# Delta-net mixer: squares ordered key first, pair scales on VectorE, two of four diagonal block copies on GpSimd, and E blocks placed ahead of the block copies into KQ

## The chip, the cores and the metric

The kernel runs on one core of a Trainium2 chip. The metric is device time in microseconds (us). The core has five instruction queues that run side by side, each strictly in its own order: PE (TensorE, the matrix engine; the profile shows its weight loads apart as PEld), DVE (VectorE), ACT (ScalarE), POOL (GpSimd) and SP (SyncE, which here only issues DMAs). An instruction that has to wait for a semaphore holds up everything that stands behind it in the same queue. [...]

## The reference

A two-layer encoder trunk over 256 positions of width 1024. Each layer is a SwiGLU block, a mixer, and a second SwiGLU block, each between RMS norms. The mixer of layer 0 is a short convolution, that of layer 1 a gated delta net. Only the delta net is touched by the change:

```python
CHUNK = 64
k_beta = k * beta[..., None]
a = jnp.where(strict, einsum("bhncd,bhnsd->bhncs", k_beta, k) * decay, 0.0)
t_inv = triangular_solve(eye + a, eye, left_side=True, lower=True)
u = einsum("bhncs,bhnse->bhnce", t_inv, v_beta)
qk = jnp.where(causal, einsum("bhncd,bhnsd->bhncs", q, k) * decay, 0.0)
...
v_new = u_n - einsum("bhcd,bhde->bhce", w_n, state)
o = einsum("bhcd,bhde->bhce", q_g_n, state) + einsum("bhcs,bhse->bhce", qk_n, v_new)
```

q and k are normalised per head (8 key heads, each used by two of the 16 value heads), so the sum of squares of each key and query row is needed; t_inv is the inverse of a unit triangular matrix for each head and each piece of the sequence. The output is the trunk's result, 256 x 1024 in float32.

## The kernel before

**Number format and units.** Products are made at float32 accuracy from a rounded part and a residual. Each weight block of 128 x 1024 (a "unit") is brought in by SP's queue (three raw buffers), rounded by ACT (`whi`, L119), and its residual made by DVE (`wlo`, L121); eight pairs of `whi` and `wlo` exist at a time. PE multiplies twice or three times per block: L221, L222 and L225 in a group of 24 matmuls with 512 columns (`act_group`), L278 to L280 in a group of 24 with 256 columns (`stat_group`).

**The delta-net stage** runs in this order of code: head slabs, then nine tiles of keys and queries (`stat_group`), three z groups (`z_group`, six tiles of 24 matmuls: 144), four v groups (`v_group`, 16 tiles), and the last z group. Other work is threaded into this as chains: Python generators that a ticker resumes every few matmuls, so that a chain's instructions are recorded between those of the large products. A list scheduler then fixes the order on each engine: from what it takes to be ready it picks what was recorded first. The order that stands in each queue in the end can therefore differ from the code's, and the order of one engine can move when another's work changes.

**`kq_chain`** (L605) goes over four groups of two key heads. For a head it transposes keys and queries on PE (L618), multiplies keys with keys and queries (L621), both into PSUM buffers named `acc` of which there are four, copies parts out on ACT (L624, L625) and makes sums of squares on ACT (L630, a square with accumulation, four for each head). For a group POOL adds a small constant (L634), DVE takes the reciprocal (L636), POOL makes the pair scales `dsc` (L639), and DVE makes eight scaled products with the decay into the tile `KQ` (L645, four for each half t of the sequence). ACT then copies the four 32 x 32 diagonal blocks of each half into `Ld` (L652, 32 copies in all). POOL makes three more small tiles from the sums (L654, L656, L658).

**`invert`** (L667) starts when all four groups are done. DVE transposes `Ld` (L669), inverts all the 32 x 32 blocks at once by 31 steps of two instructions (L677, L679), each of which needs the one before, and transposes the result twice (`Xd`, L681, and `Yd`, L683). POOL copies the inverted blocks back into `KQ` (L689, 32 copies). After `yield INV_WAIT`, the inverse of the larger blocks is built in two halves of eight heads: PE multiplies with `Xd` (L707), ACT copies out (L711), PE again (L718, L719), ACT copies into the tiles `E` and `KQ` (L722, L726), and so on to L742. `E` is filled beforehand by POOL from `Xd` (L699, L700).

**`v_pair`** and **`scan`** follow: a convolution of v on DVE (`yb`, L586), a SiLU on ACT (L573), transposes on PE (L757), and the solve with `KQ` on PE (L771).

Of the kernel before, what the change touches and what calls it, by code (L numbers as in the profile page):

```python
# [7 lines left out]
F32 = mybir.dt.float32  # L8
F32R = mybir.dt.float32r
AF = mybir.ActivationFunctionType  # L10
ALU = mybir.AluOpType
# [38 lines left out]
def trunk_kernel(ctx: ExitStack, tc: tile.TileContext, x, norm_g, w_gu, w_dn, sc_in, sc_cw, sc_out,  # L50
# [76 lines left out]
    def slab(shape, dtype, name):  # L127
        return hp.tile(shape, dtype, name=name, tag="slab")
# [347 lines left out]
    def gdn_proj(xh, xl, mid):  # L476
# [128 lines left out]
        def kq_chain():  # L605

            for gi in range(NG):
                ss = sp.tile([P, NT, 2, 2], F32, name="kss", bufs=2)
                k1 = slab([P, 2, 2, P], F32, "kq1")
                pkq = []  # L610
                for i in range(2):
                    kh = 2 * gi + i
                    while kq[kh] is None or tk.now < kq_time[kh] + KQ_WAIT:
                        yield 1
                    tp = side_bank().rearrange("p (t c) d -> p t c d", t=NT)
                    for t in range(NT):
                        for c in range(2):
                            PE.transpose(tp[:, t, c, :], kq[kh][:, c, t * P:(t + 1) * P], ident)  # L618
                    pk = side_bank().rearrange("p (t c) d -> p t c d", t=NT)
                    for t in range(NT):  # L620
                        PE.matmul(pk[:, t, :, :], lhsT=kq[kh][:, 0, t * P:(t + 1) * P],  # L621
                                  rhs=kq[kh][:, :, t * P:(t + 1) * P], start=True, stop=True)
                    pkq.append(pk)
                    S.activation(ktok[:, kh, :], tp[:, 0, 0, :], AF.Copy)  # L624
                    S.activation(k1[:, i, :, :], kq[kh][:, :, P:], AF.Copy)  # L625
                    kq1[kh] = k1[:, i, :, :]
                    for t in range(NT):
                        for c in range(2):
                            junk = sp.tile([P, 512], mybir.dt.bfloat16, name="junk", bufs=1)
                            S.activation(junk[:, 0:P], tp[:, t, c, :], AF.Square, accum_out=ss[:, t, c, i:i + 1])  # L630
                    yield 1
                while dec[1][gi] is None:
                    yield 1
                G.tensor_scalar(ss, ss, EPS, None, ALU.add)  # L634
                rk = sp.tile([P, NT, 2], F32, name="rk", bufs=2)
                V.reciprocal(rk, ss[:, :, 0, :])  # L636
                dd = small(f"dsc{gi}", 8).rearrange("p (t n) -> p t n", t=NT)
                for t in range(NT):
                    G.tensor_tensor(dd[:, t, :].rearrange("p (k v) -> p k v", k=2),  # L639
                                    beta[:, t, 4 * gi:4 * gi + 4].rearrange("p (k v) -> p k v", k=2),  # L640
                                    rk[:, t, :].unsqueeze(2).broadcast_to([P, 2, 2]), ALU.mult)
                for t in range(NT):
                    m = big([P, 4, 2, P], F32, "KQ")
                    for hv in range(4):
                        V.scalar_tensor_tensor(m[:, hv, :, :], pkq[hv // 2][:, t, :, :], dd[:, t, hv:hv + 1],  # L645
                                               bc(dec[t][gi][:, hv, :], 2), ALU.mult, ALU.mult)
                    KQ[gi][t] = m
                    for b in range(4):
                        r = slice(b * B32, (b + 1) * B32)
                        o = Ld[r, :, 8 * gi + t:8 * gi + t + 7:2].rearrange("p i v -> p v i")  # L650
                        i_ = m[r, :, 0, b * B32:(b + 1) * B32]
                        S.activation(o, i_, AF.Copy)  # L652
                n = small(f"nk{gi}", 4).rearrange("p (t n) -> p t n", t=NT)
                G.tensor_tensor(n, ss[:, :, 0, :], phalf.rearrange("p (t n) -> p t n", t=NT), ALU.pow)  # L654
                q = small(f"eq{gi}", 4).rearrange("p (t n) -> p t n", t=NT)
                G.tensor_scalar(q, ss[:, :, 1, :], 128.0 * EPS, None, ALU.mult)  # L656
                w = small(f"wt{gi}", 4)
                G.tensor_tensor(w, etail[:, 4 * gi:4 * gi + 4], dd[:, 0, :], ALU.mult)  # L658
                Dsc[gi], nk[gi], eq[gi], wt[gi] = dd, n, q, w
                yield 1  # L660
            tk.start(invert())


# [3 lines left out]
        def invert():  # L667
# [14 lines left out]
            Yd = row("blk").rearrange("p (a b) -> p a b", a=B32)  # L682
            V.transpose(Yd.rearrange("p h i -> p i h"), X)  # L683
            T1 = row("blk").rearrange("p (a b) -> p a b", a=B32)
            for gi in range(NG):
                for t in range(NT):
                    for b in range(4):
                        r = slice(b * B32, (b + 1) * B32)
                        G.tensor_copy(KQ[gi][t][r, :, 0, r], Yd[r, 8 * gi + t:8 * gi + t + 7:2, :])  # L689
            yield INV_WAIT  # L690
            for half in range(2):
                hs = slice(16 * half, 16 * half + 16)
                gis = (2 * half, 2 * half + 1)
                E = {}
                for gi in gis:
                    E[gi] = slab([P, 8, 64], F32, "E64")
                    for b in range(2):
                        r = slice(b * B32, (b + 1) * B32)
                        G.tensor_copy(E[gi][r, :, r], Xd[r, 8 * gi:8 * gi + 8, :])  # L699
                    G.memset(E[gi][0:B32, :, B32:], 0.0)  # L700
                pt = side_bank().rearrange("p a (b c) -> p (a b) c", c=B32)
                for x in range(16):
                    ht = 16 * half + x
                    m = KQ[ht // 8][ht % 2]
                    for b in (0, 2):
                        r0, r1 = slice(b * B32, (b + 1) * B32), slice((b + 1) * B32, (b + 2) * B32)
                        PE.matmul(pt[r1, x, :], lhsT=m[r0, (ht // 2) % 4, 0, r1], rhs=Xd[r0, ht, :],  # L707
                                  start=True, stop=True)
                for b in (1, 3):
                    r = slice(b * B32, (b + 1) * B32)  # L710
                    S.activation(T1[r, hs, :], pt[r], AF.Copy)  # L711
                yield 1
                py = side_bank().rearrange("p a (b c) -> p (a b) c", c=B32)
                for x in range(16):
                    ht = 16 * half + x
                    for b in (0, 2):
                        r0, r1 = slice(b * B32, (b + 1) * B32), slice((b + 1) * B32, (b + 2) * B32)
                        PE.matmul(py[r0, x, :], lhsT=T1[r1, ht, :], rhs=Yd[r1, ht, :], start=True, stop=True)  # L718
                    PE.matmul(py[B32:64, x, :], lhsT=Yd[B32:64, ht, :], rhs=T1[B32:64, ht, :], start=True, stop=True)  # L719
                for gi in gis:  # L720
                    x0 = 8 * (gi % 2)
                    S.activation(E[gi][B32:64, :, 0:B32], py[B32:64, x0:x0 + 8, :], AF.Copy, scale=-1.0)  # L722
                    for t in range(NT):
                        for b in (0, 2):
                            r0, r1 = slice(b * B32, (b + 1) * B32), slice((b + 1) * B32, (b + 2) * B32)
                            S.activation(KQ[gi][t][r0, :, 0, r1], py[r0, x0 + t:x0 + t + 7:2, :], AF.Copy, scale=-1.0)  # L726
                yield 1
                lo, up = slice(0, 64), slice(64, P)
                for gi in gis:
                    pz = side_bank().rearrange("p a (b c) -> p (a b) c", c=64)  # L730
                    for x in range(8):
                        PE.matmul(pz[up, x, :], lhsT=KQ[gi][x % 2][lo, x // 2, 0, up], rhs=E[gi][lo, x, :],
                                  start=True, stop=True)
                    S.activation(E[gi][up], pz[up], AF.Copy)
                yield 1
                for gi in gis:
                    pw = side_bank().rearrange("p a (b c) -> p (a b) c", c=64)
                    for x in range(8):
                        PE.matmul(pw[lo, x, :], lhsT=E[gi][up, x, :], rhs=KQ[gi][x % 2][up, x // 2, 0, up],
                                  start=True, stop=True)  # L740
                    for t in range(NT):
                        S.activation(KQ[gi][t][lo, :, 0, up], pw[lo, t:t + 7:2, :], AF.Copy, scale=-1.0)  # L742
                    inv_done[gi] = True
# [312 lines left out]
```

## Time and profile before

| | |
|---|---|
| median of 3 runs | 1127.42 us (1125.82 to 1130.31) |
| the profiled execution | 1128.42 us |
| its span, first to last instruction | 1126.5 us |
| DVE busy in the span | 749.9 us (67%) |
| ACT busy in the span | 651.8 us (58%) |
| POOL busy in the span | 88.8 us (8%) |
| mean granted TensorE clock | 0.995 |
| delta-net stage, from head slabs to the last z group | about 660 to 930 us of the span |

Times in the timeline are counted from the start of the span. The time of the program is 1.9 us longer than the span of the same execution, which lies ahead of the first and behind the last instruction. Durations of PE overlap, since matmuls are pipelined: how fast they go is read from the distance between starts. A bracket at the end of a timeline row gives how long the engine sat idle before that instruction, and the instruction that ended the wait.

### The profile page before, as it was taken

Reading aid. Unit: us, or ns where it says so; the run is one execution under the profiler, and the core shown is the slowest. Engines: PE = TensorE matmul, PEld = TensorE weight load, DVE = VectorE, ACT = ScalarE, POOL = GpSimd, SP = SyncE. Lnnn points to the kernel's source line nnn. Section 1 sums busy time; section 2 is a strip of 40 time slices with the busy share of each in tenths; the row PEclk is TensorE's granted clock in tenths of the full one; section 3 lists DMA queues with packets and bytes.
Section 4 is the critical chain, followed back from the end, with each engine's and each line's share of the span. In section 5 each row is a group of like instructions: output and inputs, shape, how many; then the busy total and the mean of one; then the engine's idle time right before and its main releaser. Section 6 shows DMA issues by size and latency. Waiting matters only on the chain.

```text
span 1126.5 us, 16842 instructions
## 1 busy us (share of the span) xinstructions
PE 1100.2 (98%) x6284; PEld 942.4 (84%) x6284; DVE 749.9 (67%) x1140; ACT 651.8 (58%) x1201; POOL 88.8 (8%) x167
## 2 busy tenths in 40 slices
PE   9999999999999999999999999889899999999997
PEld 6888887888788888788888877778899887888886
DVE  7776735687777663577765468768946557767543
ACT  6666535545556653556664358784587645666432
POOL 0100000000200000010000012110141212000000
PEclk9999999999999999999999999999999999999999
DMA  8755555656566565576555653327332355655552
GB/s 271 244 185 190 191 166 167 225 180 198 182 223 204 171 206 165 163 229 209 189 185 169 193 185 113 94 94 227 114 129 76 131 168 168 213 199 190 185 168 75
DMA packets 55955, 198.12 MB, mean 176 GB/s; under 512 B 6721, under 2 KB 7233, under 8 KB 55874
## 3 DMA queue, kind: packets, MB, share of 16 engines
q1 hardware_dynamic: 55728, 196.99, 54.2%
q8 instruction: 49, 0.80, 0.3%
q14 instruction: 32, 0.26, 0.1%
q10 hardware_dynamic: 146, 0.07, 0.0%
HBM read 195.99 MB, written 1.05 MB: 175 GB/s over the span
## 4 chain that ended last, share of the span: by engine, by line
PE 81%; DVE 7%; ACT 5%; DMA 3%; issue 2%; POOL 2%; SPq 0%; DVEq 0%; POOLq 0%; ACTq 0%
PE mm L298 27%; PE mm L301 14%; PE acc L324 7%; PE acc L325 7%; PE acc L323 7%; PE mm L221 3%; PE mm L222 3%; PE mm L225 3%; DVE wlo L121 2%; ACT whi L119 1%; ACT blk L652 1%; DVE kq L586 1%; PE mm L176 1%; ACT junk L147 1%; DMA raw<-in_w_gu 1%
## 5 line engine op out<-in xcount | busy, mean ns | idle before, releaser
L121 DVE TENSOR_TENSOR wlo<-raw,whi 128x1024 fp32r<-128x1024 f32 (+2 forms) x362 | 437.5, 1220 | 240.2 <-ACT whi L119 201.5
L119 ACT ACTIVATE whi<-raw 128x1024 fp32r<-128x1024 f32 (+2 forms) x362 | 376.1, 1051 | 224.3 <-PE acc L325 104.6
L298 PE MATMUL mm<-x,whi 128*128 128x512 f32 x1312 | 329.4, 393 | 0.0
L298 PEld LDWEIGHTS mm<-x,whi 128*128 128x128 f32 x1312 | 235.9, 189 | 42.4
L301 PEld LDWEIGHTS mm<-x,wlo 128*128 128x128 f32 x1312 | 179.0, 190 | 12.8
L301 PE MATMUL mm<-x,wlo 128*128 128x256 f32 x1312 | 182.9, 282 | 0.0
L323 PE MATMUL acc<-whi,hb 128*128 128x512 f32 x352 | 136.5, 388 | 0.0
L324 PE MATMUL acc<-wlo,hb 128*128 128x512 f32 x352 | 135.6, 385 | 0.3 <-DVE wlo L121 0.3
L325 PE MATMUL acc<-whi,hb 128*128 128x512 f32 x352 | 135.3, 385 | 0.0
L308 ACT ACTIVATE corr<-mm 128x256 f32<-128x256 f32 x164 | 61.2, 376 | 67.4 <-PE mm L301 65.6
L221 PE MATMUL mm<-whi,x 128*128 128x512 f32 (+1 forms) x240 | 94.4, 394 | 0.9 <-ACT x L178 0.7
L222 PE MATMUL mm<-wlo,x 128*128 128x512 f32 (+1 forms) x240 | 94.2, 393 | 0.7 <-DVE wlo L121 0.7
L225 PE MATMUL mm<-whi,x 128*128 128x512 f32 (+1 forms) x240 | 87.8, 389 | 0.2 <-DVE x L179 0.2
L324 PEld LDWEIGHTS acc<-wlo,hb 128*128 128x128 f32 x352 | 66.2, 188 | 13.8 <-DVE wlo L121 0.8
L323 PEld LDWEIGHTS acc<-whi,hb 128*128 128x128 f32 x352 | 66.2, 188 | 13.1
L325 PEld LDWEIGHTS acc<-whi,hb 128*128 128x128 f32 x352 | 66.1, 188 | 13.2
L154 POOL TENSOR_SCALAR rstd<-ss 128x1 f32<-128x1 f32 x24 | 12.3, 513 | 786.1 <-ACT junk L147 786.1
L278 PE MATMUL mm<-x,whi 128*128 128x256 f32 x200 | 59.7, 299 | 2.0 <-DVE kq L586 2.0
L279 PE MATMUL mm<-x,whi 128*128 128x256 f32 x200 | 58.4, 292 | 0.0
L280 PE MATMUL mm<-x,wlo 128*128 128x256 f32 x200 | 57.9, 289 | 0.0
L222 PEld LDWEIGHTS mm<-wlo,x 128*128 128x128 f32 x240 | 45.2, 188 | 11.2 <-DVE wlo L121 2.9
L221 PEld LDWEIGHTS mm<-whi,x 128*128 128x128 f32 x240 | 45.2, 188 | 11.1 <-ACT x L178 2.7
(216 smaller groups left out, 1238.3 us busy)
## 6 DMA issues: line engine op xcount, KB each, us to landing
raw<-in_w_gu SPq DMA_DIRECT2D x176, 512.0 KB, 4.2
raw<-in_w_dn SPq DMA_DIRECT2D x88, 512.0 KB, 3.6
raw<-in_sc_in SPq DMA_DIRECT2D x24, 512.0 KB, 4.1
raw<-in_gdn_z SPq DMA_DIRECT2D x16, 512.0 KB, 3.9
raw<-in_gdn_v SPq DMA_DIRECT2D x16, 512.0 KB, 4.2
raw<-in_gdn_out SPq DMA_DIRECT2D x16, 512.0 KB, 3.7
gamma<-in_norm_g SPq DMA_DIRECT2D x11, 512.0 KB, 5.4
raw<-in_gdn_a SPq DMA_DIRECT2D x9, 512.0 KB, 4.4
```

The costliest lines, as they stand in the source:

```text
L119: S.activation(hi[:, r], raw[:, r], AF.Copy)
L121: newest[0] = V.tensor_tensor(lo[:, r], raw[:, r], hi[:, r], ALU.subtract).ins
L221: PE.matmul(pt, lhsT=xh[:, t, k, :], rhs=hi, start=(k == 0), stop=False)
L222: PE.matmul(pt, lhsT=xh[:, t, k, :], rhs=lo, start=False, stop=False)
L225: PE.matmul(pt, lhsT=xl[:, t, j, :], rhs=part(j)[0], start=False, stop=(j == KD - 1))
L278: PE.matmul(ptile, lhsT=hi, rhs=h2, start=(k == 0), stop=False)
L298: PE.matmul(flat, lhsT=part(k, 0), rhs=xx[:, k].rearrange("p h t q -> p (h t q)"), start=(k == 0), stop=False)
L301: PE.matmul(flat[:, T:], lhsT=part(k, 1), rhs=xx[:, k, 0].rearrange("p t q -> p (t q)"), start=False, stop=(k == KD - 1))
L308: S.activation(c, pt[:, 1, :], AF.Copy)
L323: PE.matmul(o, lhsT=yh(c, t), rhs=hi[:, r], start=(c == 0), stop=False)
L324: PE.matmul(o, lhsT=yh(c, t), rhs=lo[:, r], start=False, stop=False)
L325: i = PE.matmul(o, lhsT=yl(c, t), rhs=hi[:, r], start=False, stop=(c == n - 1)).ins
```

## The change

Four edits, all in `gdn_proj`:

1. In `kq_chain` the sums of squares stand ahead of the two copies out of PSUM, and both key squares (c = 0) ahead of both query squares (c = 1). The tile `ss` has its axes swapped, so that the key sums lie together.
2. Adding the small constant to the key sums and making the pair scales `dsc` move from POOL to DVE. The query sums get the constant in the instruction that makes `eq`.
3. Of the four diagonal block copies of each half, ACT keeps two and POOL makes two: 16 copies and 16 copies.
4. In `invert` the copies into `E` are recorded ahead of the copies into `KQ`, half by half, with an explicit order on POOL's queue; before, all 32 copies into `KQ` were recorded first.

```diff
-                ss = sp.tile([P, NT, 2, 2], F32, name="kss", bufs=2)
+                ss = sp.tile([P, 2, NT, 2], F32, name="kss", bufs=2)
...
+                    for c in range(2):
+                        for t in range(NT):
+                            junk = sp.tile([P, 512], mybir.dt.bfloat16, name="junk", bufs=1)
+                            S.activation(junk[:, 0:P], tp[:, t, c, :], AF.Square, accum_out=ss[:, c, t, i:i + 1])
                     S.activation(ktok[:, kh, :], tp[:, 0, 0, :], AF.Copy)
                     S.activation(k1[:, i, :, :], kq[kh][:, :, P:], AF.Copy)
                     kq1[kh] = k1[:, i, :, :]
-                    for t in range(NT):
-                        for c in range(2):
-                            junk = sp.tile([P, 512], mybir.dt.bfloat16, name="junk", bufs=1)
-                            S.activation(junk[:, 0:P], tp[:, t, c, :], AF.Square, accum_out=ss[:, t, c, i:i + 1])
...
-                G.tensor_scalar(ss, ss, EPS, None, ALU.add)
+                V.tensor_scalar(ss[:, 0], ss[:, 0], EPS, None, ALU.add)
                 rk = sp.tile([P, NT, 2], F32, name="rk", bufs=2)
-                V.reciprocal(rk, ss[:, :, 0, :])
+                V.reciprocal(rk, ss[:, 0])
                 dd = small(f"dsc{gi}", 8).rearrange("p (t n) -> p t n", t=NT)
                 for t in range(NT):
-                    G.tensor_tensor(dd[:, t, :].rearrange("p (k v) -> p k v", k=2),
+                    V.tensor_tensor(dd[:, t, :].rearrange("p (k v) -> p k v", k=2),
...
-                        S.activation(o, i_, AF.Copy)
+                        if b < 2:
+                            S.activation(o, i_, AF.Copy)
+                        else:
+                            G.tensor_copy(o, i_)
...
-                G.tensor_scalar(q, ss[:, :, 1, :], 128.0 * EPS, None, ALU.mult)
+                G.tensor_scalar(q, ss[:, 1], EPS, 128.0 * EPS, ALU.add, ALU.mult)
...
-            for gi in range(NG):
-                for t in range(NT):
-                    for b in range(4):
-                        r = slice(b * B32, (b + 1) * B32)
-                        G.tensor_copy(KQ[gi][t][r, :, 0, r], Yd[r, 8 * gi + t:8 * gi + t + 7:2, :])
+            E, placed = {}, [None]
+
+            def place(half):
+
+                gis = (2 * half, 2 * half + 1)
+                for gi in gis:
+                    E[gi] = slab([P, 8, 64], F32, "E64")
...
+                            G.tensor_copy(E[gi][r, :, r], Xd[r, 8 * gi:8 * gi + 8, :])
...
+                                last = G.tensor_copy(KQ[gi][t][r, :, 0, r], Yd[r, 8 * gi + t:8 * gi + t + 7:2, :]).ins
+                placed[0] = last
+
+            place(0)
             yield INV_WAIT
             for half in range(2):
...
+                if half:
+                    place(1)
```

**What the edits move in the queues.** The scheduler gives other orders on PE, ACT, DVE and POOL through the whole delta-net stage; SP's is the same. Three places matter. Line numbers of the changed kernel are up to 16 higher: L723 is the old L707, L684 and L686 the old L681 and L683, L680 and L682 the old L677 and L679, L653 and L655 the old L652, L727 the old L711, L773 and L787 the old L757 and L771.

First PE, where the first products with the inverted blocks stand (`acc<-blk,KQ`). Before, they stand in the v groups (L278 to L280), behind all 144 matmuls of the z groups and 228 of the v groups:

```order
L278 MATMUL mm<-x_5783,whi 128x256
L279 MATMUL mm<-x_5783,whi 128x256
L280 MATMUL mm<-x_5783,wlo 128x256
L707 MATMUL acc<-blk,KQ 32x32 x32
L278 MATMUL mm<-x_5783,whi 128x256
L279 MATMUL mm<-x_5783,whi 128x256
```

Of the change, the same engine and products: they stand ahead of the last tile of the three z groups (L221 to L225).

```order
L221 MATMUL mm<-whi,x_5783 128x512
L222 MATMUL mm<-wlo,x_5783 128x512
L225 MATMUL mm<-whi,x_5783 128x512
L723 MATMUL acc<-blk,KQ 32x32 x32
L221 MATMUL mm<-whi,x_5783 128x512
L222 MATMUL mm<-wlo,x_5783 128x512
```

So 24 matmuls of 512 columns, 228 of 256 columns and three sets of four transposes of v (old L757) have moved from ahead of these products to behind them. What they wait for is the first transpose of the inverse on DVE (old L681).

Second DVE in the middle of the inversion (`blk` and `sg`). Before, the convolutions of v (`yb`) and the residuals (`wlo`) stand between its steps, 20 and 18 of them up to the first transpose of the result:

```order
L677 TENSOR_TENSOR sg<-blk 128x247
L586 SCALAR_TENSOR_TENSOR yb<-mm,gcw,yb 128x255
L679 TENSOR_TENSOR blk<-blk,sg 128x13x19
L586 SCALAR_TENSOR_TENSOR yb<-mm,gcw,yb 128x254
L677 TENSOR_TENSOR sg<-blk 128x240
L586 SCALAR_TENSOR_TENSOR yb<-mm,gcw,yb 128x253
```

Of the change, the end of the inversion on DVE:

```order
L680 TENSOR_TENSOR sg<-blk 128x31
L682 TENSOR_TENSOR blk<-blk,sg 128x31
L684 STREAM_TRANSPOSE blk<-blk 128x32x32
L686 STREAM_TRANSPOSE blk<-blk 128x32x32
L121 TENSOR_TENSOR wlo<-raw,whi 128x1024 x4
L586 SCALAR_TENSOR_TENSOR yb<-mm,gcw,yb 128x255
```

The convolutions of v now all stand behind the inversion, and of the residuals eight stand inside it, all in its first ten steps.

Third ACT, from the last head's squares (`junk,kss`) to the end of the z groups' SiLUs (`zs`). Before:

```order
L573 ACTIVATE zs<-mm 128x512
L119 ACTIVATE whi<-raw 128x1024
L652 ACTIVATE blk<-KQ 32x4x32 x4
L119 ACTIVATE whi<-raw 128x1024
L652 ACTIVATE blk<-KQ 32x4x32 x4
L119 ACTIVATE whi<-raw 128x1024
L573 ACTIVATE zs<-mm 128x512
```

Of the change:

```order
L119 ACTIVATE whi<-raw 128x1024
L653 ACTIVATE blk<-KQ 32x4x32 x2
L119 ACTIVATE whi<-raw 128x1024
L653 ACTIVATE blk<-KQ 32x4x32 x2
L119 ACTIVATE whi<-raw 128x1024 x7
L573 ACTIVATE zs<-mm 128x512 x4
L727 ACTIVATE blk<-acc 32x512 x2
L119 ACTIVATE whi<-raw 128x1024 x3
```

The copy out of the first products (L727) now stands ahead of the next three roundings of weights.

More of the change, by code (lines that the diff above doesn't have):

```diff
@@ L651, in kq_chain @@
                         i_ = m[r, :, 0, b * B32:(b + 1) * B32]
-                        S.activation(o, i_, AF.Copy)
+                        if b < 2:
+                            S.activation(o, i_, AF.Copy)
+                        else:
+                            G.tensor_copy(o, i_)
                 n = small(f"nk{gi}", 4).rearrange("p (t n) -> p t n", t=NT)
-                G.tensor_tensor(n, ss[:, :, 0, :], phalf.rearrange("p (t n) -> p t n", t=NT), ALU.pow)
+                G.tensor_tensor(n, ss[:, 0], phalf.rearrange("p (t n) -> p t n", t=NT), ALU.pow)
                 q = small(f"eq{gi}", 4).rearrange("p (t n) -> p t n", t=NT)
-                G.tensor_scalar(q, ss[:, :, 1, :], 128.0 * EPS, None, ALU.mult)
+                G.tensor_scalar(q, ss[:, 1], EPS, 128.0 * EPS, ALU.add, ALU.mult)
                 w = small(f"wt{gi}", 4)
@@ L684, in invert @@
             T1 = row("blk").rearrange("p (a b) -> p a b", a=B32)
-            for gi in range(NG):
-                for t in range(NT):
-                    for b in range(4):
-                        r = slice(b * B32, (b + 1) * B32)
-                        G.tensor_copy(KQ[gi][t][r, :, 0, r], Yd[r, 8 * gi + t:8 * gi + t + 7:2, :])
+            E, placed = {}, [None]
[3 more added lines that the diff above has]
+                    E[gi] = slab([P, 8, 64], F32, "E64")
+                    for b in range(2):
+                        r = slice(b * B32, (b + 1) * B32)
+                        with tc.issue_after(placed[0]) if placed[0] else nullcontext():
+                            G.tensor_copy(E[gi][r, :, r], Xd[r, 8 * gi:8 * gi + 8, :])
+                    with tc.issue_after(placed[0]) if placed[0] else nullcontext():
+                        last = G.memset(E[gi][0:B32, :, B32:], 0.0).ins
+                placed[0] = last
+                for gi in gis:
+                    for t in range(NT):
+                        for b in range(4):
+                            r = slice(b * B32, (b + 1) * B32)
+                            with tc.issue_after(placed[0]):
+                                last = G.tensor_copy(KQ[gi][t][r, :, 0, r], Yd[r, 8 * gi + t:8 * gi + t + 7:2, :]).ins
+                placed[0] = last
+            place(0)
             yield INV_WAIT
@@ L693, in invert @@
                 gis = (2 * half, 2 * half + 1)
[L694 to L697, printed above, removed]
-                        r = slice(b * B32, (b + 1) * B32)
-                        G.tensor_copy(E[gi][r, :, r], Xd[r, 8 * gi:8 * gi + 8, :])
-                    G.memset(E[gi][0:B32, :, B32:], 0.0)
+                if half:
+                    place(1)
                 pt = side_bank().rearrange("p a (b c) -> p (a b) c", c=B32)
```

## The prediction

> **What bounds the kernel now.** I read the page's busy shares first, then the view of waits for PE's queue, then the timeline of PE around its longest waits, then the windows of the granted clock.
>
> ```profile
> PE 1100.2 (98%) x6284; PEld 942.4 (84%) x6284; DVE 749.9 (67%) x1140; ACT 651.8 (58%) x1201; POOL 88.8 (8%) x167
> PE acc L618 <- ACT kq L573: 3.6, 2, 3.1
> PE mm L757 <- ACT yb L573: 3.4, 1, 3.4
> ...
> PE acc L621 <- DVE KQ L645: 1.7, 1, 1.7
> PE acc L707 <- DVE blk L681: 0.2, 1, 0.2
> ```
>
> PE sets the end: it is busy for 98% of the span, so time is lost or won only where PE waits. The rows of waits (total, times, longest, in us) that lie in the change's reach are these four: 3.6, 3.4, 1.7 and 0.2. The last row is the one to keep in mind. Products with the inverted blocks (L707) wait for the first transpose of the inverse on DVE (L681), and now they wait 0.2 us. The timeline gives the places:
>
> ```profile
> 746.69 1.12 PE L618 MATMUL acc<-ident,kq 128*128 128x128 f32 x4 [3.06 <-ACT kq L573]
> 794.53 1.12 PE L757 MATMUL mm<-ident,yb 128*128 128x128 f32 x4 [3.41 <-ACT yb L573]
> 812.06 1.20 PE L707 MATMUL acc<-blk,KQ 32*32 32x32 f32 x64 [0.18 <-DVE blk L681]
> ...
> 746.00:748.00 2.00, 1.31 (x5) 1.25 (x6) 1.51 (x2) 1.21 (x5) 0.00 (x0) 0.64 0.88 248
> 748.00:750.00 2.00, 2.00 (x6) 1.60 (x5) 0.06 (x1) 1.49 (x9) 0.25 (x2) 0.51 0.90 303
> ```
>
> The windows' column behind the five engines is the granted clock: after the wait of 3.06 us PE ran at about half speed, 0.64 and 0.51 in two windows of 2 us, so (0.36 + 0.49) x 2 = 1.7 us were lost on top of it.
>
> **The sum has three terms**: when the inversion starts on DVE, how long it takes there in its new company, and how much of PE's work the new order has put behind it.
>
> **First term: the start.** In the profile the transpose of `Ld` starts at 758.02.
>
> ```profile
> L652 ACT ACTIVATE blk<-KQ 32x128 f32<-32x128 f32 x32 | 13.8, 430 | 2.3 <-DVE KQ L645 2.0
> 735.00:750.00 15.00, 11.41 (x58) 9.60 (x57) 10.44 (x20) 13.48 (x39) 2.25 (x8) 0.89 0.34 110
> 749.67 0.24 POOL L634 TENSOR_SCALAR kss<-kss 128x8 f32<-128x8 f32 x1 [12.43 <-ACT junk L630]
> 749.99 1.04 POOL L654 TENSOR_TENSOR nk<-kss,phalf 128x4 f32<-128x4 f32 x1
> 751.65 3.23 DVE L645 SCALAR_TENSOR_TENSOR KQ<-acc,dsc,dec 128x256 f32<-128x256 f32 x8 [1.53 <-POOL dsc L639]
> 748.41 0.28 ACT L630 ACTIVATE junk<-acc 128x128 bf16<-128x128 f32 x1
> 748.81 0.28 ACT L630 ACTIVATE junk<-acc 128x128 bf16<-128x128 f32 x1
> 756.18 1.80 ACT L652 ACTIVATE blk<-KQ 32x128 f32<-32x128 f32 x4
> 758.02 1.25 DVE L669 STREAM_TRANSPOSE blk<-blk 128x1024 f32<-128x1024 f32 x1 [2.01 <-ACT blk L652]
> ```
>
> ACT is busy for 13.48 of 15 us in that stretch, so what leaves its queue counts nearly in full. Of the 32 copies at 430 ns, 24 stand ahead of the last head's SiLU, and 12 of these go: 5.2 us. About 1.4 us of it I give back: in the new PE order the whole first z tile, 24 matmuls and not 21, stands ahead of the last head's transposes, and its last residual comes behind eight products and five convolution steps on DVE. Then the scales of the last group: now 2.0 us pass from the sums (749.67) to the products (751.65), POOL's 1.04 us power among them. Afterwards the two key squares suffice, two squares earlier (0.4 us apart, 748.41 and 748.81); four small DVE instructions, at the 0.18 us of the nearest row below, follow, and one residual (1.14 us) stands between them: 1.9 us. That saves 0.9. Last, from the products to the end of the copies now 758.0 - 751.65 = 6.3 us pass; eight products (3.2 us) and two copies (0.9 us) are 4.1, which saves 2.2. POOL makes its two meanwhile. In all 5.2 - 1.4 + 0.9 + 2.2 = 6.9 us, start **751.1**. Bounds: if nothing comes of the shorter ACT queue and only the 0.9 us is won, 757.1; if nothing is given back (1.4) and ACT's idle time goes too (2.3 ahead of these copies, 1.5 in the window of 15 us), 745.9.
>
> **Second term: the length.** From 758.02 to 812.0 are 54.0 us. Grouped rows of that window on DVE, and two pieces of its timeline:
>
> ```profile
> L636 DVE RECIPROCAL rk<-kss 128x4 f32<-128x4 f32 x4 | 0.7, 176 | 6.3 <-POOL kss L634 6.3
> L121 DVE TENSOR_TENSOR wlo<-raw,whi 128x1024 fp32r<-128x1024 f32 x18 | 21.9, 1217 | 2.0 <-ACT whi L119 1.7
> L679 DVE TENSOR_TENSOR blk<-blk,sg 128x31 f32<-128x31 f32 (+15 forms) x31 | 10.4, 337 | 0.4
> L677 DVE TENSOR_TENSOR sg<-blk 128x31 f32<-128x31 f32 (+15 forms) x31 | 10.4, 336 | 0.4
> L586 DVE SCALAR_TENSOR_TENSOR yb<-mm,gcw,yb 128x255 f32<-128x255 f32 (+2 forms) x20 | 9.5, 474 | 0.9 <-ACT yb L584 0.8
> 771.42 0.38 DVE L677 TENSOR_TENSOR sg<-blk 128x207 f32<-128x207 f32 x1
> 771.84 0.38 DVE L679 TENSOR_TENSOR blk<-blk,sg 128x207 f32<-128x207 f32 x1
> 772.13 1.22 DVE L121 TENSOR_TENSOR wlo<-raw,whi 128x1024 fp32r<-128x1024 f32 x1
> 773.26 0.38 DVE L677 TENSOR_TENSOR sg<-blk 128x220 f32<-128x220 f32 x1
> ...
> 788.53 0.42 DVE L679 TENSOR_TENSOR blk<-blk,sg 128x252 f32<-128x252 f32 x1
> 788.99 0.42 DVE L677 TENSOR_TENSOR sg<-blk 128x247 f32<-128x247 f32 x1
> 789.32 0.48 DVE L586 SCALAR_TENSOR_TENSOR yb<-mm,gcw,yb 128x255 f32<-128x255 f32 x1
> 789.71 0.41 DVE L679 TENSOR_TENSOR blk<-blk,sg 128x247 f32<-128x247 f32 x1
> ```
>
> A residual between two steps stretches their distance from 0.42 to 1.42 us (771.84 to 773.26): 1.0 us each. A convolution step stretches 0.46 to 0.72: 0.27 each. The new order keeps 8 of 18 residuals and none of 20 convolution steps: 54.0 - 10 x 1.0 - 20 x 0.27 = 38.6. Most of the 2.0 us idle of the first row should go too. From below: transpose 1.2, steps 10.4 + 10.4 + 62 x 0.04 between a step's end and the next start, residuals 8.0, last transpose 2.2: 34.7. I take 36.7, in the middle: the blocks are there at 751.1 + 36.7 = **787.8**, 24 us earlier than now.
>
> **Third term: what PE has behind it.** In the queue of before, 144 z matmuls and 228 v matmuls stood ahead of L707, so DVE's 54 us were covered by them to within 0.2 us. In the new queue its successor L723 stands right behind 96 matmuls that follow the last head. The last head's transposes come 5.2 - 1.4 us ahead of 746.69, and at the pace of the rows below 96 matmuls take 21.8 us: PE is there near 765, over 20 us before the blocks, and an in-order queue cannot take what stands behind. From 787.8 on PE still has to do what it had done by 812.06: 24 matmuls of 0.227 us, 228 of 0.12 us and three sets of transposes of 0.44 us, 5.4 + 27.4 + 1.3 = 34.1 us.
>
> ```profile
> 751.70 0.39 PE L221 MATMUL mm<-whi,x 128*128 128x512 f32 x1
> 754.19 0.39 PE L225 MATMUL mm<-whi,x 128*128 128x512 f32 x1
> ...
> 719.01 0.28 PE L278 MATMUL mm<-x,whi 128*128 128x256 f32 x1
> 721.17 0.28 PE L278 MATMUL mm<-x,whi 128*128 128x256 f32 x1
> 802.38 0.44 PE mm L757 x4
> ```
>
> (Eleven steps between the first two rows, 18 between the next two.) The shift is 787.8 + 34.1 - 812.06 = +9.8 us. The waits of 3.6, 1.7 and 3.4 us go or no longer matter, since PE only comes sooner to the one long wait: they are in the sum already. The restart from the long wait costs 1.7 us at half clock, as above, since it is longer than the wait that showed it: 9.8 + 1.7 = **+11.5 us**.
>
> [...]
>
> **Edits that cost nothing.** The order of the squares moves `ktok` and `kq1` copies by 1.6 us on ACT; the PSUM buffer is freed by the same five readers. 12 small instructions more on DVE, 2 us, lie in its 4.6 us of idle time in that 15 us window; if that cover were gone, they would delay the start by 0.5 us per group. E ahead of KQ on POOL: the view of PE's waits lists none for them now, and with 34 us of PE work ahead of their use they stay covered. SP's queue is unchanged.
>
> **Rivals.** (1) *The other side, faster:* the inversion is done before PE comes to L723, so that only the removed waits count: 3.6 + 3.4 + 1.7 + 0.2 and 2 x 1.7 of clock, 12.3 us, 1115. It decides at 766, which needs a start near 729, 22 us ahead of where the last group's products start now (751.65). 4%. (2) *Almost even:* both terms at their short bounds, start 745.9 and length 34.7: blocks at 780.6, 7.2 us sooner than forecast, +4.3, 1131.7. 10%. (3) *The change doesn't do what it says:* products and copies are held by something other than ACT and POOL, start 757.1: +17.5, 1145. 11%. (4) *POOL's copies are slow* where DVE runs residuals:
>
> ```profile
> 827.98 0.39 POOL L699 COPY E<-blk 32x256 f32<-32x256 f32 x1
> 828.77 2.67 POOL L699 COPY E<-blk 32x256 f32<-32x256 f32 x2
> 828.63 2.56 DVE L121 TENSOR_TENSOR wlo<-raw,whi 128x1024 fp32r<-128x1024 f32 x2 [3.93 <-ACT whi L119]
> ```
>
> The same copy took 0.39 us alone and 1.33 us beside a residual. One residual follows the last products, so the last two copies could hold the start by 1 to 3 us: about 1141. 15%. [...]
>
> **How the numbers follow.** The forecast, 60%: 1128.42 + 11.5 = 1139.9 against the profiled execution, which lies 1.0 above the median of three, so **1138.9**. Its own spread, 2 us each for start and length, is 1135 to 1143. The range, 1132 to 1145, takes in (4), half of (2) and of (3). A measurement can tell about 0.5%, 5.6 us: faster is (1), 4%; the same is most of (2), 8%; slower the rest, 88%.
>
> **What would show it.** In the changed profile the view of PE's waits is led by L723 <- DVE L684, about 20 us; L672 starts near 751 and L684 ends near 788; the granted clock is at half behind the wait; no wait of PE at L773. It is wrong if L723 waits below 10 us, or if the v groups behind it wait for residuals or convolutions that DVE has put off, which would make it slower than the range.

## The result and the profile after

The changed kernel takes **1141.51 us** (median of four runs, 1141.44 to 1141.81) against 1128.87 us of the kernel before on the same chip (1125.82 to 1131.11): a ratio of **1.0114 with a 95% interval of 1.0087 to 1.0141**, so it is slower by 1.1%. The prediction was 1138.9 us, in a range of 1132 to 1145.

The profiled execution of the change took 1141.49 us with a span of 1139.8 us, 13.3 us more than the span of before. The page's row of busy time and the row of the granted clock in 40 slices (tenths of full speed):

```profile
PE 1100.0 (97%) x6284; PEld 942.8 (83%) x6284; DVE 755.7 (66%) x1152; ACT 644.7 (57%) x1185; POOL 96.0 (8%) x171
...
PEclk9999999999999999999999999995999999999999
```

PE does the same 6284 matmuls in the same 1100 us; the span has grown around them, and one slice out of 40, from 769.4 to 797.9, shows a granted clock of 5 tenths. The view of waits for PE's queue (total us, times, longest) of the change names the cause in its first row:

```profile
PE acc L723 <- DVE blk L684: 21.4, 1, 21.4
...
PE acc L621 <- ACT ktok L628: 1.0, 1, 1.0
...
PE mm L773 <- ACT yb L573: 0.3, 1, 0.3
```

The 0.2 us that the products with the inverted blocks waited before have become 21.4. The waits of 3.1 us at L618 and of 3.4 us at L757 (now L773) are gone or down to 0.3. The 1.7 us at L621 are 1.0 now, and the instruction waited for is another: the `ktok` copy, which the first edit put behind the squares. The timeline of the change shows the chain:

```profile
709.57 0.41 PE L278 MATMUL mm<-x,whi 128*128 128x256 f32 x1 [1.96 <-DVE kq L586]
...
749.14 0.89 POOL L655 COPY blk<-KQ 32x128 f32<-32x128 f32 x2 [0.75 <-DVE KQ L645]
750.50 1.22 DVE L121 TENSOR_TENSOR wlo<-raw,whi 128x1024 fp32r<-128x1024 f32 x1
750.64 1.81 POOL L655 COPY blk<-KQ 32x128 f32<-32x128 f32 x2 [0.61 <-DVE KQ L645]
752.49 1.25 DVE L672 STREAM_TRANSPOSE blk<-blk 128x1024 f32<-128x1024 f32 x1 [0.78 <-POOL blk L655]
786.58 2.03 DVE L684 STREAM_TRANSPOSE blk<-blk 128x1024 f32<-128x1024 f32 x1
788.66 1.92 PE L723 MATMUL acc<-blk,KQ 32*32 32x32 f32 x64 [21.35 <-DVE blk L684]
849.67 2.05 PE L787 MATMUL acc<-nv,KQ 128*128 128x128 f32 x16
```

For comparison two rows of the timeline of before, one from ahead of all that the change touches and one from behind it:

```profile
707.50 0.39 PE L278 MATMUL mm<-x,whi 128*128 128x256 f32 x1 [1.97 <-DVE kq L586]
...
836.44 2.05 PE L771 MATMUL acc<-nv,KQ 128*128 128x128 f32 x16
```

The first row is a clock mark. The same wait of 2 us for the same convolution lies at 707.50 in one execution and at 709.57 in the other, so 2.07 us of the difference in span were there before the change had done anything. In the eleven profiled executions of this study that mark lies between 707.5 and 710.7 us, though ahead of it the same instructions ran in the same order on every engine (in one kernel a single fill of a tile on POOL came early). Times are therefore compared below from this mark on ("behind the mark"). From the mark to the end, before takes 1126.5 - 707.50 = 419.0 us and the change 1139.8 - 709.57 = 430.2: **+11.2 us**. At the first solve with `KQ` (L771, now L787) the shift is 849.67 - 836.44 - 2.07 = 11.2 us already, so all of it arises between the two rows, and nothing more comes behind.

What DVE does in the change from the start of the inversion to the end of the first transpose (groups of DVE's instructions from 752.4 to 788.7; busy us, mean ns, idle us ahead):

```profile
L682 DVE TENSOR_TENSOR blk<-blk,sg 128x31 f32<-128x31 f32 (+15 forms) x31 | 10.6, 343 | 1.0
L680 DVE TENSOR_TENSOR sg<-blk 128x31 f32<-128x31 f32 (+15 forms) x31 | 10.6, 342 | 0.9
L121 DVE TENSOR_TENSOR wlo<-raw,whi 128x1024 fp32r<-128x1024 f32 x8 | 9.7, 1217 | 1.0 <-ACT whi L119 0.8
```

All 62 steps, eight residuals, no convolution: 788.61 - 752.49 = 36.1 us where before took 54.0. The inversion is earlier and shorter than it was, and yet PE stands still, since its queue brings it there 21 us too soon. The windows of the change at the restart (after the window's bounds and length: busy us of PE, PEld, DVE, ACT, POOL, then granted clock, DMA share, GB/s):

```profile
788.00:790.00 2.00, 1.34 (x50) 1.35 (x52) 2.00 (x2) 0.00 (x0) 1.18 (x4) 0.50 0.00 0
790.00:792.00 2.00, 2.00 (x26) 1.65 (x23) 0.35 (x1) 1.18 (x2) 1.78 (x6) 0.50 0.00 0
792.00:794.00 2.00, 2.00 (x6) 1.60 (x5) 0.00 (x0) 0.48 (x1) 1.72 (x7) 0.50 0.00 0
794.00:796.00 2.00, 2.00 (x8) 1.56 (x7) 1.23 (x1) 0.84 (x2) 1.84 (x4) 0.72 0.00 0
```

From the restart at 788.66 PE lost 0.67 + 1.0 + 1.0 + 0.56 = 3.2 us at half clock.

### The profile page after: what moved, and what is told of

It is laid out like the page before. It is cut to its first block, busy times and chain, and to the rows that moved or that the text cites. A ratio compares the mean times of both kernels' runs of the same rounds, so it can differ in the third digit from the quotient of the medians.

```text
span 1139.8 us, 16876 instructions
## 1 busy us (share of the span) xinstructions
PE 1100.0 (97%) x6284; PEld 942.8 (83%) x6284; DVE 755.7 (66%) x1152; ACT 644.7 (57%) x1185; POOL 96.0 (8%) x171
## 5 line engine op out<-in xcount | busy, mean ns | idle before, releaser
L221 PE MATMUL mm<-whi,x 128*128 128x512 f32 (+1 forms) x240 | 96.9, 404 | 0.6 <-ACT x L178 0.5
L225 PE MATMUL mm<-whi,x 128*128 128x512 f32 (+1 forms) x240 | 89.0, 393 | 0.0
L278 PE MATMUL mm<-x,whi 128*128 128x256 f32 x200 | 59.0, 295 | 2.0 <-DVE kq L586 2.0
L280 PE MATMUL mm<-x,wlo 128*128 128x256 f32 x200 | 57.7, 289 | 0.0
L221 PEld LDWEIGHTS mm<-whi,x 128*128 128x128 f32 x240 | 46.0, 192 | 11.0 <-ACT x L178 2.4
```

Source lines behind the costliest of these rows:

```text
L221: PE.matmul(pt, lhsT=xh[:, t, k, :], rhs=hi, start=(k == 0), stop=False)
L225: PE.matmul(pt, lhsT=xl[:, t, j, :], rhs=part(j)[0], start=False, stop=(j == KD - 1))
L278: PE.matmul(ptile, lhsT=hi, rhs=h2, start=(k == 0), stop=False)
```

## The experiments

The theory: the fourth edit takes the two E64 slabs of the first half, and records the copies that fill them, ahead of the point where the inversion's chain gives way; by this the products with the inverted blocks move forward in PE's queue, and DVE's inversion runs in one piece, while the first three edits are a gain by themselves. The main rival: the third and second edits load POOL and DVE, and cost what is lost (in the profile of before a copy of POOL took 0.39 us alone and 1.33 us beside a residual of DVE). Nine kernels ran, in three groups, each beside runs of the kernel before on its chip (medians 1130.79, 1130.80 and 1130.54).

| kernel | median us | ratio, 95% interval | PE's wait at the products | transpose of `Ld`, behind the mark |
|---|---|---|---|---|
| before | 1128.87 | 1 | 0.2 us | 50.5 us |
| full change | 1141.51 | 1.0114 (1.0087 to 1.0141) | 21.4 | 42.9 |
| edits 1 to 3 | 1119.95 | 0.9901 (0.9884 to 0.9917) | none | 42.9 |
| edit 4 alone | 1149.99 | 1.0168 (1.0150 to 1.0186) | 22.9 | 50.4 |
| full, `place(0)` one line later | 1120.12 | 0.9906 (0.9886 to 0.9925) | none | 42.9 |
| full, products held on PE | 1134.05 | 1.0032 (1.0022 to 1.0043) | none | 41.4 |
| full, E64 in its own buffers | 1120.45 | 0.9910 (0.9887 to 0.9933) | none | 42.9 |
| edits 1 and 2 | 1128.52 | 0.9978 (0.9965 to 0.9991) | none | 50.2 |
| edit 3 alone | 1124.28 | 0.9951 (0.9931 to 0.9970) | 0.2 | 44.3 |
| edits 1, 2, 4 | 1149.23 | 1.0162 (1.0143 to 1.0180) | 22.0 | 50.2 |
| edits 1, 3, 4, scales on POOL | 1141.58 (one run) | - | 23.1 | 44.9 |

### The fourth edit undone

```diff
-            place(0)
             yield INV_WAIT
...
-                if half:
-                    place(1)
+                E = {}
+                for gi in gis:
+                    E[gi] = slab([P, 8, 64], F32, "E64")
```

The 32 copies into `KQ` stand ahead of the yield again, as before. The expectation:

> The changed kernel with the fourth edit undone (copies into E and KQ recorded as before); the squares, the pair scales and the block copies stay changed. Theory A (the loss comes from the order that the fourth edit brings about): the products with the inverted blocks stand late in PE's queue again, their wait on DVE is below 2 us, DVE's inversion is again mixed with convolutions and residuals, and the time is that of before or better, since PE's waits of 3.1 us (key transposes) and 1.7 us and the half clock behind them (1.7 us) have lost their cause: 1119 to 1126 us. Rival B (the copies on POOL and the scales on DVE cost the time, through DVE's and POOL's shared time): at least 1131 us, with new waits of PE in the key stage or at the products with the inverted blocks.

Measured: 1119.95 us, within the theory's range. The view of PE's waits of this kernel, and rows of its timeline (L710 and L760 are the full change's L723 and L773):

```profile
PE mm L760 <- ACT yb L573: 2.0, 2, 1.7
PE mm L221 <- ACT x L178: 1.7, 1, 1.7
```

```profile
752.50 1.25 DVE L672 STREAM_TRANSPOSE blk<-blk 128x1024 f32<-128x1024 f32 x1 [0.78 <-ACT zs L573]
800.91 2.23 DVE L684 STREAM_TRANSPOSE blk<-blk 128x1024 f32<-128x1024 f32 x1
803.71 1.20 PE L710 MATMUL acc<-blk,KQ 32*32 32x32 f32 x64
```

The inversion starts at the same time as in the full change (752.50 and 752.49), takes 50.6 us instead of 36.1 up to the end of its first transpose, and the blocks are 14.5 us later than there (803.14 against 788.61). PE comes to the products 0.6 us after that and does not wait. A faster inversion was not what the kernel lacked. From the mark (709.58) to the end (1118.1) are 408.5 us, 10.5 less than before and 21.7 less than the full change: **the fourth edit costs 21.7 us on top of the other three**, about its wait of 21.4 us. The half clock behind that wait, 3.2 us, stands against the waits of 2.0 and 1.7 us above, which the full change does not have. The rival falls.

### The fourth edit alone

The kernel before with `place` as in the diff of the change, and nothing else of it.

> The kernel before with the fourth edit alone. Theory A: PE waits for the first transpose of the inverse 20 to 28 us, the inversion stands unmixed on DVE and takes 35 to 38 us, and since its start is not brought forward by the other edits (758 to 760 us in the span, not 751) the time is above the full change: 1143 to 1150 us. Rival B (the fourth edit is harmless by itself): 1125 to 1132 us with a wait below 2 us.

Measured: 1149.99 us, at the upper end of the theory's range. Rows of its timeline:

```profile
709.36 0.58 PE L278 MATMUL mm<-x,whi 128*128 128x256 f32 x1 [2.09 <-DVE kq L586]
...
759.79 1.25 DVE L669 STREAM_TRANSPOSE blk<-blk 128x1024 f32<-128x1024 f32 x1 [2.00 <-ACT blk L652]
...
797.45 1.92 PE L720 MATMUL acc<-blk,KQ 32*32 32x32 f32 x64 [22.94 <-DVE blk L681]
```

The start lies 50.4 us behind the mark, as before the change (50.5), and the blocks are 797.40 - 759.79 = 37.6 us later. Against the full change the start is 7.5 us later behind the mark and the end 9.5 us (1149.1 - 709.36 = 439.7 against 430.2); 1.5 us of the rest lie in the inversion itself, 37.6 us where the full change took 36.1. Where PE waits for the inversion, the other edits are worth little more than what they bring its start forward; what they gain elsewhere is lost in the wait.

### One line moved

```diff
-            place(0)
             yield INV_WAIT
+            place(0)
```

> The full change with one line moved: the first half's copies into E and KQ are recorded behind the point where the chain gives way to other work, not ahead of it. E still goes ahead of KQ. Theory A: nothing is recorded ahead of that point but the two transposes, the products with the inverted blocks stand late in PE's queue, and the time is that of the run with the fourth edit undone, within 3 us: 1118 to 1126 us. Rival B (E ahead of KQ on POOL is what costs): as the full change, 1138 to 1145 us.

Measured: 1120.12 us, like the run with the fourth edit undone. In its timeline the blocks are there at 804.94 and the products follow at 805.45 without a wait:

```profile
802.69 2.25 DVE L684 STREAM_TRANSPOSE blk<-blk 128x1024 f32<-128x1024 f32 x1
...
805.45 1.20 PE L723 MATMUL acc<-blk,KQ 32*32 32x32 f32 x64
```

So E ahead of KQ on POOL, and the explicit order there, cost nothing; the loss hangs on whether the first half is placed ahead of the yield or behind it. Against the kernel before this version wins 0.9%, as much as leaving the edit out.

### PE's order restored, DVE's left

The full change, but the products may not stand on PE ahead of the large matmul recorded last before them:

```diff
+                held = main[0]
...
-                        PE.matmul(pt[r1, x, :], lhsT=m[r0, (ht // 2) % 4, 0, r1], rhs=Xd[r0, ht, :],
-                                  start=True, stop=True)
+                        with tc.issue_after(held):
+                            PE.matmul(pt[r1, x, :], lhsT=m[r0, (ht // 2) % 4, 0, r1], rhs=Xd[r0, ht, :],
+                                      start=True, stop=True)
```

> The full change, but on PE the products with the inverted blocks are told to stand behind the large matmul that was recorded last before them; DVE's order stays that of the change (inversion in one piece, with its steps ahead of the residuals and convolutions). Theory A (two locks: PE's order and DVE's order): PE no longer waits 21 us at the products with the inverted blocks, but residuals and convolutions that DVE has put off behind the inversion are late now, and PE waits for those near 785 to 800 us instead, 8 to 20 us in all: 1128 to 1138 us. Rival (PE's position alone makes the loss): no wait above 4 us, 1116 to 1123 us.

Measured: 1134.05 us, in the middle of the theory's range and far from the rival's. PE's waits at the two lines concerned, the wait of SP's queue for residuals from 768 to 800 us, and the rows of the timeline that show where they come from (L775 is the full change's L773):

```profile
PE mm L775 <- ACT yb L573: 8.1, 2, 7.7
PE mm L280 <- DVE wlo L121: 5.3, 1, 5.3
SPq L113 <- DVE wlo L121: 25.5, 4, 21.4
```

```profile
788.44 1.91 DVE L686 STREAM_TRANSPOSE blk<-blk 128x1024 f32<-128x1024 f32 x1
790.17 3.74 DVE L121 TENSOR_TENSOR wlo<-raw,whi 128x1024 fp32r<-128x1024 f32 x3
791.51 0.58 PE L280 MATMUL mm<-x,wlo 128*128 128x256 f32 x1 [5.27 <-DVE wlo L121]
...
795.12 1.06 ACT L119 ACTIVATE whi<-raw 128x1024 fp32r<-128x1024 f32 x1 [19.13 <-DMA raw<-in_gdn_v]
...
797.39 1.50 DVE L586 SCALAR_TENSOR_TENSOR yb<-mm,gcw,yb 128x255 f32<-128x255 f32 x3
...
801.73 1.12 PE L775 MATMUL mm<-ident,yb 128*128 128x128 f32 x4 [7.72 <-ACT yb L573]
```

The wait of 21 us is gone, and two others of 5.3 and 7.7 us have come: a residual and a convolution that stand behind the second transpose of the inversion on DVE. More than DVE's order is behind the second. The residuals put off also hold the raw weight buffers, so that SP's queue waited 21.4 us for one of them before it could bring in the next block, ACT stood 19.1 us for that block, and DVE 2.3 us for ACT. There are **two locks, not one**. (The start 41.4 us behind the mark, 1.5 less than in the full change, is no gain of the edit: the granted clock behind the wait at the mark was 1.00 in this execution, as the last section shows.) The prediction saw the first and named the second as something that would make it wrong; it lies hidden behind the first in the full change.

### E64 in buffers of its own

```diff
-NSMALL = 22
+NSMALL = 20
...
-                    E[gi] = slab([P, 8, 64], F32, "E64")
+                    E[gi] = sp.tile([P, 8, 64], F32, name="E64", bufs=2)
```

> The full change, with the first half's and second half's copies recorded where the change records them, but the tiles E64 taken from two buffers of their own instead of the shared ring of slabs, which has 20 instead of 22 buffers of its size class to make room. Theory A (the order comes from E64 being taken out of the shared ring ahead of slabs that z and v work need): the products with the inverted blocks stand late again, no wait above 3 us at them, 1117 to 1125 us. Rival (the position of the copies in the code, or their explicit order on POOL, brings the loss): 1138 to 1145 us.

Measured: 1120.45 us. The copies are recorded as in the full change, ahead of the yield; only the place in memory differs, and the ring is shorter by the two buffers. In its timeline:

```profile
803.44 2.23 DVE L684 STREAM_TRANSPOSE blk<-blk 128x1024 f32<-128x1024 f32 x1
...
806.19 1.20 PE L723 MATMUL acc<-blk,KQ 32*32 32x32 f32 x64
```

Blocks at 805.67, products at 806.19, no wait. So neither the position of the copies in the code nor their order on POOL moved the queues: the two slabs did that, taken from the shared ring ahead of those of the z and v work. With 20 buffers in the ring and E64 still in it, the products stand early in PE's queue as in the full change, right behind 96 matmuls that follow the last head; that is read from its queue order, since the variant was not run.

How two slabs do this can be followed in the order of the programs. It is not that z or v work waits for a buffer that E64 frees: the next to use the two buffers are a v slab and a tile of the scan, the same two tiles in the kernel before and in the full change. It is the turn in the ring. In the full change the five z slabs asked for behind the two E64 slabs are first written right behind the first write of the second of these, a copy out of `Xd`, and so behind the inversion. With `place(0)` one line later, or with E64 in its own buffers, all five are first written ahead of the inversion's end. The z tiles come out of PE into four PSUM buffers (`mm`). One tile whose SiLU has its slab, and four that fill these buffers, are the 120 z matmuls that still stand ahead of the products; the last z tile and the v groups, which need a buffer from these four, stand behind. The counts fit, but that the scheduler weighed it so is argued, since no run shows its choice itself.

### The parts of the gain

Edits 1 and 2 without 3 and 4, and then edit 3 alone:

```diff
-                        if b < 2:
-                            S.activation(o, i_, AF.Copy)
-                        else:
-                            G.tensor_copy(o, i_)
+                        S.activation(o, i_, AF.Copy)
```

These lines, shown against the full change, undo the third edit for the first kernel, in which the fourth is undone too, as above. The second kernel is the one before with the removed lines put in and nothing else.

> Before with the first two edits alone (order of the squares, scales on VectorE); ACT makes all 32 block copies. Theory: what frees PE from its wait of 3.1 us at the key transposes (L618) is the shorter ACT queue of the third edit, so it stays at 2 to 3 us here with its half clock: 1124 to 1130 us. Rival: the scales on VectorE (0.9 us sooner for each group) and the order of the squares do it, or POOL's copies slow the rest: 1118 to 1122 us.

> Before with the third edit alone (16 of 32 block copies on POOL). Theory: the eight copies of the third group that stand ahead of the last head's SiLU become four, 1.7 us less on ACT, so PE's wait of 3.1 us at L618 falls to about 1.4 us and the half clock behind it is gone: 1122 to 1127 us. Rival: the copies on POOL run beside VectorE at 0.9 us and more each and hold the key stage, so the wait stays: 1128 us or more.

Measured: 1128.52 us and 1124.28 us, both within the theories' ranges. The rows of PE's waits at the key transposes, first with edits 1 and 2, then with edit 3:

```profile
PE acc L618 <- ACT kq L573: 3.5, 1, 3.5
...
PE acc L618 <- ACT ktok L628: 1.9, 1, 1.9
```

```profile
PE acc L618 <- ACT kq L573: 0.3, 1, 0.3
```

The wait of 3.1 us goes with the third edit and stays (3.5, where 2 to 3 were expected) without it; that it fell to 0.3 and not to the 1.4 expected is more than was worked out. The row of 1.9 us was not expected: an earlier head's transposes wait for a PSUM buffer whose last reader is now the `ktok` copy, where before has 0.5 us at L618 for a square. The prediction put the new order of the squares at nothing. With edit 3 beside it that wait is gone, and 1.0 us at L621 for the same copy is left; how much of the 1.9 us is the order's and how much the block copies' was not tested. In ratios the parts give 0.9978 and 0.9951, which multiply to 0.9929, and together they measure 0.9901 (0.9884 to 0.9917). The 0.3% between the two is about as wide as the three intervals leave open, so that the edits gain more together than apart is not shown.

### The parts of the start

Two more kernels take one edit out of the full change, to price the terms of the start. The first is the diff above on the full change; the second is this:

```diff
-                V.tensor_scalar(ss[:, 0], ss[:, 0], EPS, None, ALU.add)
+                G.tensor_scalar(ss[:, 0], ss[:, 0], EPS, None, ALU.add)
...
-                    V.tensor_tensor(dd[:, t, :].rearrange("p (k v) -> p k v", k=2),
+                    G.tensor_tensor(dd[:, t, :].rearrange("p (k v) -> p k v", k=2),
```

> The full change with the third edit undone: ACT makes all 32 block copies. It prices the copies' share of the start, since the end moves one for one with the start of the inversion as long as PE waits for it. Theory (first term of the prediction: 12 copies of 0.43 us ahead of the last head's SiLU, and four copies in ACT's queue behind the last products in place of two): the transpose of Ld starts 5 to 7 us later than in the full change, measured from PE's wait at L278 near 709 us, and the time is 1146 to 1149 us. Rival (POOL's copies beside VectorE's residuals eat what ACT saves): at most 3 us later, 1141 to 1144 us.

> The full change with the constant and the pair scales left on POOL (second edit half undone). Theory (scales' share of the start was put at 0.9 us, and PE's order puts six more large matmuls, 1.4 us, ahead of the last head's transposes): the transpose of Ld starts 1 to 3 us later than in the full change, 1142 to 1145 us. Rival (the scales hide behind something else): start within 0.5 us of the full change, 1140 to 1142 us.

Measured: 1149.23 us for the first, just above the range given. Its timeline:

```profile
709.29 0.39 PE L278 MATMUL mm<-x,whi 128*128 128x256 f32 x1 [1.96 <-DVE kq L586]
...
759.47 1.25 DVE L669 STREAM_TRANSPOSE blk<-blk 128x1024 f32<-128x1024 f32 x1 [2.98 <-ACT blk L652]
```

The start is 50.2 us behind the mark and 7.3 later than in the full change, 0.3 above the upper end expected. The second kernel, one run, took 1141.58 us, 0.4 below the 1142 expected and so in the rival's range. Its rows put the start 44.9 us behind the mark, 2.0 later than the full change, as the theory had it and not the rival:

```profile
708.32 0.39 PE L278 MATMUL mm<-x,whi 128*128 128x256 f32 x1 [1.97 <-DVE kq L586]
...
753.21 1.25 DVE L672 STREAM_TRANSPOSE blk<-blk 128x1024 f32<-128x1024 f32 x1 [1.13 <-ACT blk L653]
```

The end behind the mark is 8.3 us later in the first (1147.8 - 709.29 = 438.5) and 1.4 later in the second (431.6): close to one for one with the start.

## Why the prediction was right, step by step

**The bound.** PE's queue sets the end, and the one row of 0.2 us that the prediction asked the reader to keep in mind became the 21.4 us that lead the list. PE came to L723 at 788.66 - 21.35 = 767.3, or 765.2 less the 2.07 us of the mark, where 765 was worked out. Undoing its cause took away 21.7 us.

**The start** was put at 751.1, and came at 752.49, that is 750.4 with the 2.07 us of the mark taken off: 7.6 us earlier than before where 6.9 were worked out. Its parts differ from the working. The copies on ACT are nearly all of it: taking only the third edit out of the full change gives back 7.3 of the 7.6 us, and edit 3 alone brings 6.2 (44.3 behind the mark against 50.5), while the prediction put 5.2 - 1.4 of the ACT queue and 2.2 behind the products to this edit, 6.0 in all. The 0.9 us of the scales cannot be told from these runs: their kernel starts 2.0 us later, but with six more matmuls, 1.4 us, ahead of the last head in PE's order.

**The length** was put at 36.7 us between 34.7 and 38.6, and is 36.1. Steps (10.6 + 10.6 us), residuals (eight) and convolutions (none) are as the queue order said.

**The blocks** are there at 788.61, or 786.5 less the 2.07 us, where 787.8 was forecast: 1.3 us sooner, 0.7 of it from the start and 0.6 from the length.

**The half clock at the restart is the term that was mis-sized**: 1.7 us in the sum, 3.2 measured, since the clock stayed at half until 795.1, 6.5 us past the restart. The prediction took the 1.7 us behind the wait of 3.06 us in the trace of before for the longer wait too; that was its estimate. The kernel with the fourth edit alone, whose wait was 22.9 us, lost 3.8 us counted the same way: its clock stayed at half until 805.0, 7.5 us past the restart. Its window in which the clock came back (half up to 805.0, full behind it):

```profile
804.00:806.00 2.00, 2.00 (x8) 0.76 0.35 41
```

**The work behind the wait** was put at 34.1 us. From the products to the first solve, the change takes 849.67 - 788.66 = 61.0 us and before 836.44 - 812.06 = 24.4; of the difference of 36.6 us 3.2 are the half clock, which leaves 33.4, 0.7 less than worked out. So the blocks erred by -1.3 us, the half clock by +1.5 and the work by -0.7. That these nearly cancel, and +11.2 us were measured where +11.5 were forecast, is luck.

**The waits that go** are nothing here, as the prediction said, because PE only comes sooner to the long one. They are far from nothing where that wait is missing: without the fourth edit the kernel is 10.8 us faster than before by the medians, where rival 1, in which only the removed waits count, had worked out 12.3.

**Rival 4, POOL's copies beside a residual**, came true in part: the last two copies took 1.81 us beside DVE's residual where the two ahead of them took 0.89, and ended at 752.45, ACT's own at 751.85. They held the start by some 0.6 us, less than the 1 to 3 us of the rival. A caution on reading: the same start is put down to `POOL blk L655` in the trace of the full change and to `ACT zs L573` in that without the fourth edit, with the same POOL copies ending at 752.45 and 752.46. The SiLU of a z tile has no part in `Ld`; it only ended at nearly the same moment. A releaser's name is worth a look at what else ended then.

**The level.** The forecast stood on a median of 1127.42 us for before, and the runs beside the change gave 1128.87. That is 1.4 of the 2.6 us by which 1138.9 is too low.

## What to carry to other kernels

An operation that is made ready earlier is worth nothing if the consumer had not waited for it (0.2 us here), and a queue that brings the consumer forward turns the old cover into a wait (21.4 us here): before a change of order, compare for each in-order queue when its engine reaches the moved instruction and when the operand is there, and count the work that has moved behind it. A buffer taken earlier from a shared ring can change the order of everything that shares the ring, on engines that the edit never names; taking it one line later, or from a pool of its own, gave 1.9% here. Undoing one edit of several is the quickest test: three of these four were a gain of 1.0% that the fourth hid.

## What the runs showed that was not expected

**A wait of PE of 2 to 3.5 us cost between nothing and about 3 us of half clock on top.** The wait of 2.0 us at the mark, in the same code, was followed by some 1.7 us lost at half clock in ten of the eleven profiled executions, that of before among them, and by none in the run with the products held. Windows of before, and then of that run, where the wait ended at 710.68 (after the bounds and the length: PE busy, granted clock, DMA share, GB/s):

```profile
708.00:710.00 2.00, 2.00 (x15) 0.75 0.32 47
710.00:712.00 2.00, 2.00 (x11) 0.50 0.72 268
712.00:714.00 2.00, 2.00 (x15) 0.89 0.54 197
```

```profile
708.00:710.00 2.00, 0.71 (x4) 1.00 0.00 0
710.00:712.00 2.00, 1.32 (x11) 1.00 0.00 0
```

At the other end, a wait of 3.2 us that ended at 791.06 in the run of edit 3 alone kept the clock at half until about 796.7, for 5.7 us past the restart:

```profile
790.00:792.00 2.00, 0.94 (x5) 0.50 0.00 0
792.00:794.00 2.00, 2.00 (x11) 0.50 0.55 154
794.00:796.00 2.00, 2.00 (x11) 0.50 0.27 109
796.00:798.00 2.00, 2.00 (x16) 0.82 0.82 252
```

That is 0.47 + 1.0 + 1.0 + 0.36 = 2.8 us lost, where before, counted the same way, lost 1.6 us each after waits of 3.06 and 3.41 us. The run of edits 1 and 2 lost 3.0 us after its wait of 3.5 us, and nothing after one of 2.1 us further on. A sum over one profile's half clock is thus good to a microsecond or two for each such wait. Why the same wait was free in one execution and not in another is open: no run here shifted a wait by a known amount.
